# A hybrid attention layer on one core: another order of Strassen products, a last gate with priority, a plain last down-projection, and operands at equal addresses modulo 256

## The chip, the cores and the metric

The kernel runs on one core of a Trainium2 chip. A core has five engines with a queue of instructions each: TensorE (matmuls; the profile shows them as PE, and the loads of their stationary operands as PEld), VectorE (DVE), ScalarE (ACT), GpSimd (POOL, not used here) and SyncE (SP), whose queue issues the DMAs. They run side by side and wait for each other by semaphores. TensorE reads its two operands from SBUF, 128 partitions wide, and writes sums to PSUM, which has eight banks of 2 KB a partition.

The metric is the time of one execution on the device in microseconds; lower is better. One further execution was recorded by the hardware profiler, and every trace row is from that one.

## What is computed

One layer on 256 tokens of width 2048, in float32: RMS norm, an input projection, two kinds of attention with eight heads of 128 each, an output projection with a residual, then a gated feed-forward network (FFN) with a causal convolution of width 3 over the tokens. The change concerns the FFN, and the addresses in all of it:

```python
def conv_ffn(h, w_up_l, conv_w_l, conv_b_l, w_down_l):
    u = h @ w_up_l                        # 2048 -> 2 x 5632
    ...                                   # causal depthwise convolution, width 3, plus bias
    gate, val = jnp.split(u, 2, axis=-1)
    return (jax.nn.silu(gate) * val) @ w_down_l      # 5632 -> 2048

x = x + hybrid_mixer(h, ...)
x = x + conv_ffn(rms_norm(x, ffn_norm), ...)
```

## The kernel before

**Precision.** A float32 operand `a` is split into a high part `hi`, rounded to the matmul type `float32r`, and `lo = a - hi`. A product takes three matmuls: hi by hi, hi by lo, lo by hi. For weights, `split` (lines 204 to 213) makes `w_hi` with an ACT cast (line 208) and `w_lo` with a DVE subtraction (line 209). Every weight byte goes through both engines.

**The matmuls.** `token_major` (line 222) takes activations as the stationary operand, 128 tokens at a time, and 512 columns of weights as the moving one (lines 237 to 239). `feature_major` (line 244) takes the weights as stationary and `hT`, the normalized input transposed and split, as moving: for each of 16 slices of the input and two blocks of features one matmul of 512 columns (line 252, `hi` against both parts of `hT`) and one of 256 (line 257). It comes in two halves of eight slices, each with one load of 1 MB and one split. After each half it calls `step()`.

**The FFN.** 44 tiles of 128 features are worked on in six parts (line 40): four tiles in the first, eight in each of the others. A part goes through its tiles two at a time (lines 783 to 795): `up_pair` for the gate and for the value, each a `feature_major` and a `convolved` (line 596). `convolved` sums the PSUM parts (`t2`, lines 268 and 269), multiplies by the token factors into `up` (line 602), and forms the three taps: an ACT instruction (line 606) and two DVE ones (line 611) for each of the two tiles. Then silu (line 787), the product with the value (line 788), and the split of the result into `g2` (lines 790 and 791). One `g2` holds two tiles; a part of eight tiles has four pairs. From the third pair on, `combinations` (line 642) makes sums `s` of two pairs' gates on DVE and ACT.

**The down-projection of a part** is done while the next part's up-projections run. `down_in_seven` (line 664) is one step of Strassen's method in Winograd's form on blocks of four tiles by 512 columns and 128 tokens: seven products of 12 matmuls each (line 681) instead of eight, at the price of sums of weights on DVE (lines 719, 726, 732 and 743), of the activations (`s`), and of more additions to the residual (line 692). It is a generator; each `yield` ends a product. Its first product, `bank_c`, takes pairs 2 and 3 (the second half of the part's tiles), its second, `bank_a`, pairs 0 and 1, the others `s` of all pairs, the last pairs 2 and 3. Two such blocks cover 2048 columns. `step()` (line 621) hands them out: with a pace of 14 a half of an up-projection is followed by 14/16 of a product on average, the first product of a part coming after the second half. The first part has two pairs and goes through `down_plain` (line 749), the usual product of 24 matmuls for four tiles by 512 columns and both token blocks (lines 764 to 766, added at line 770).

**The last part** has no up-projection to run beside. Lines 803 to 806 deal out its down-projection by hand: `heavy`, seven products for columns 0 to 1023, and `light`, plain products for columns 1024 to 2047.

**Order.** TensorE's instructions run in the order in which they are written (`manual_schedule`, line 776). For the other engines a list scheduler fixes the order when the program is built; an instruction's place in the text is its priority, and `tc.high_priority(offset=n)` moves it ahead by `n` places. Weight loads and splits are moved ahead by `AHEAD` = 200, `t2`, the gate's product, `g2`, `combinations` and the residual's additions by 400. The instructions of `convolved` from line 602 on are not moved.

**Addresses.** Tiles lie in pools, one pool behind another, each tile rounded up to 32 bytes a partition. In the attention stage the pools behind `at` are `tmp`, `wraw`, `whi`, `wlo`, `late`; in the FFN the order is `wlo2`, `whi2`, `wraw2`, `wsum`, `ff`. Pools `at` and `wlo2` start at the same byte. The byte addresses of operands in a partition, before:

| tile | pool | address | modulo 256 | modulo 512 |
|---|---|---|---|---|
| `hT` (both stages; also holds `oT12` to `oT15`) | `big` | 37984 | 96 | 96 |
| `w_hi`, attention (first buffer; others 8192 on) | `whi` | 155424 | 32 | 288 |
| `w_lo`, attention | `wlo` | 171808 | 32 | 288 |
| `oT0` to `oT11` (attention outputs; steps of 2048) | `late` | 188192 | 32 | 288 |
| `w_lo`, FFN | `wlo2` | 73312 | 96 | 96 |
| `w_hi`, FFN | `whi2` | 97888 | 96 | 96 |
| `g2` (eight, steps of 4096) | `ff` | 179872 | 160 | 160 |
| `s` (two) | `ff` | 212640 | 160 | 160 |

Two things put them there: `lf`, 64 bytes in `at`, ahead of the pools behind it, with 128 bytes for `la` in `tmp`; and the two tiles `up`, 2080 bytes each, that lie in `ff` ahead of `t2`, the gates, `g2` and `s`. Slices of these operands are taken at multiples of 512 bytes, except in the three value projections of 344 columns, whose rows are 1376 bytes.

Of the kernel before, what the change touches and what calls it, by code (L numbers as in the profile page):

```python
# [2 lines left out]

# [40 lines left out]
def hybrid_layer(  # L44
# [227 lines left out]
    with ExitStack() as actx:  # L272
# [101 lines left out]
        step()  # L374

        vA = at.tile([P, NT, WF], F32, name="vA")
        lf = at.tile([P, NT, NH], F32, name="lf")
        for j in range(3):
            acc = project(2 * WF + 344 * j, 344)
            n = 344 if j < 2 else 336  # L380
# [197 lines left out]
    wraw = ctx.enter_context(tc.tile_pool(name="wraw2", bufs=4))  # L578
    wsum = ctx.enter_context(tc.tile_pool(name="wsum", bufs=1))
    ff = ctx.enter_context(tc.tile_pool(name="ff", bufs=2))  # L580
    psf = ctx.enter_context(tc.tile_pool(name="psf", bufs=2, space=bass.MemoryType.PSUM))
    crow = ff.tile([NC2, 4, P], F32, name="crow", tag="val", bufs=1)
    nc.sync.dma_start(crow[:, :3, :], conv_w[0].rearrange("w (n p) -> n w p", p=P))
    nc.sync.dma_start(crow[:, 3, :], conv_b[0].rearrange("(n p) -> n p", p=P))
    up = [ff.tile([P, 2, 2 + S], F32, name=f"up{i}", bufs=1) for i in range(2)]
    for u in up:
        dve.memset(u[:, :, 0:2], 0.0)
    n_up = 0
# [7 lines left out]
    def convolved(ps, f0, tag, bufs):  # L596

        nonlocal n_up
        u = up[n_up % 2]
        n_up += 1  # L600
        t2 = summed(ff, ps, "t2")
        dve.tensor_tensor(u[:, :, 2:], t2, R.unsqueeze(1).to_broadcast([P, 2, S]), op=ALU.mult)
        a = ff.tile([P, 2, S], F32, name=tag, tag=tag, bufs=bufs)
        for j in range(2):
            f = f0 + j
            act.activation(  # L606
                a[:, j, :], u[:, j, 2:], AF.Identity,
                scale=ccol[:, 2, f : f + 1], bias=ccol[:, 3, f : f + 1],
            )
            for w in range(2):  # L610
                dve.scalar_tensor_tensor(  # L611
                    a[:, j, :], u[:, j, w : w + S], ccol[:, w, f : f + 1], a[:, j, :],
                    op0=ALU.mult, op1=ALU.add,
                )
        return a
# [14 lines left out]
            else:  # L630
                n_behind -= 16

    def up_pair(f0, tag, bufs):

        nonlocal R
        acc = feature_major(wu, f0 * P, psa, "acc")
        if R is None:
            R = in_every_partition(dg2, 2, const)
            convolution_parameters()
        return convolved(acc, f0, tag, bufs)  # L640

    def combinations(g1, g2):

# [17 lines left out]
    def store(t, c0):  # L661
        nc.sync.dma_start(of[t * P : (t + 1) * P, c0 : c0 + 512], xt[t][:, c0 : c0 + 512])

    def down_in_seven(f0, pairs, sums, c0, final=False):


        w11, w12 = (rows_of(wd, f0, 4, c0 + i * 512, 512) for i in range(2))
# [15 lines left out]
                        stop=i == 3 and n == 2, skip_group_check=not first,  # L683
                    )

        adds = {}

        def add(t, half, bank, op=ALU.add):
            c = c0 + 512 * half
            to = xt[t][:, c : c + 512]  # L690
            with tc.high_priority(offset=2 * AHEAD):
                dve.tensor_tensor(to, to, bank, op=op)  # L692

            adds[t, half] = adds.get((t, half), 0) + 1
            if final and adds[t, half] == (1 if (t, half) == (1, 0) else 2):
                store(t, c)

        def ahead():
            return tc.high_priority(offset=AHEAD)

        bank_c = psb.tile([P, 512], F32, name="bank_c", tag="t")
        with ahead():
            parts = split(load(w21), 4, 512)
        product(bank_c, True, of_pairs(1, 0), parts)
        add(0, 0, bank_c)
        yield
        bank_a = psf.tile([P, 512], F32, name="bank_a", tag="a")
        with ahead():
            b11 = load(w11)
            parts = split(b11, 4, 512)  # L710
        product(bank_a, True, of_pairs(0, 0), parts)
        add(0, 0, bank_a)
        yield

        bank_b = psb.tile([P, 512], F32, name="bank_b", tag="t")
# [61 lines left out]
    for n_part, (f_lo, f_hi) in enumerate(FFN_PARTS):  # L777
        last_part = n_part == len(FFN_PARTS) - 1
        pairs, gates, sums = [], [], []
        n_behind = 0  # L780

        pace = 4 if n_part == 1 else 14
        for f in range(f_lo, f_hi, 2):
            gate = up_pair(f, "gate", 3)
            val = up_pair(NFT + f, "val", 1)
            with tc.high_priority(offset=2 * AHEAD):
                act.activation(gate, gate, AF.Silu)
                dve.tensor_tensor(gate, gate, val, op=ALU.mult)
                g2 = ff.tile([P, 2, 2, S], F32R, name="g2", tag="g2", bufs=8)
                act.copy(g2[:, 0], gate)  # L790
# [12 lines left out]
    heavy = down_in_seven(f_lo, pairs, sums, 0, final=True)  # L803
    light = down_plain(f_lo, pairs, 1024, 1024, final=True)
    for g in (light, heavy, light, heavy, heavy, light, heavy, heavy, heavy, light, heavy):
        next(g)


def _constants():
# [54 lines left out]
```

## Time and profile before

| | |
|---|---|
| time before, median of 3 runs | 1177.89 us (1177.38 to 1179.56) |
| the profiled execution | 1177.3 us, of which 1175.5 us from its first to its last instruction (the span) |
| granted TensorE clock over the span | 0.985 |
| busy: TensorE, VectorE, ScalarE | 1134.4, 906.3, 614.6 us |
| read from HBM, written | 217.80 MB, 2.10 MB (187 GB/s) |

A row of instructions in a list by time has its start and duration in us, the engine, the line, the operation, `out<-in` by the program's names, shapes, and how many follow each other; in brackets the idle time before it and what ended it. Times are from the span's start. Matmuls overlap, and a matmul's duration is a model's; the spacing of their starts tells the rate. A row of waits has the engine and line that waited, `<-` what it waited for, the total in us, how often, and the longest. In rows of groups the last columns are busy time, mean ns of one, and idle time before. "PEclk" is the granted share of TensorE's clock.

### The profile page before, as it was taken

What the parts mean: (1) busy time and instruction counts of PE and PEld (TensorE: products, weight loads), DVE (VectorE), ACT (ScalarE), POOL (GpSimd) and SP (SyncE); (2) the same over time, 40 slices, a digit from 0 to 9 for tenths busy, and PEclk for the clock granted to TensorE, in tenths of its full rate; (3) what the DMA queues carried; (4) which work ended last, traced back from release to release, by engine and by line L of the source; (5) the groups of instructions that cost most, each with busy time, mean ns of one, the idle gap of its engine ahead of it and who ended that gap; (6) DMA issues with size and microseconds to landing.
All of it is one profiled execution on the core that took longest, in us unless ns stands there. A gap on an engine that the chain in (4) does not pass through costs nothing.

```text
span 1175.5 us, 14481 instructions
## 1 busy us (share of the span) xinstructions
PE 1134.4 (97%) x5894; PEld 963.9 (82%) x5894; DVE 906.3 (77%) x982; ACT 614.6 (52%) x667; POOL 0.2 (0%) x4
## 2 busy tenths in 40 slices
PE   7999999999999989999999998999989998999967
PEld 5998888888888878888888887888878887888846
DVE  4646656455465676767899999989998999889985
ACT  5644445445563564554555565555545565555542
POOL 0000000000000000000000000000000000000000
PEclk9999999999999999999999999999989998999979
DMA  7665545554445395555557565575737566474732
GB/s 231 212 219 180 179 146 177 179 156 166 144 144 179 109 292 179 186 198 190 181 174 253 181 220 199 189 222 197 239 131 236 193 223 206 144 251 158 260 104 86
DMA packets 167292, 220.83 MB, mean 188 GB/s; under 512 B 3880, under 2 KB 117690, under 8 KB 167226
## 3 DMA queue, kind: packets, MB, share of 16 engines
q1 hardware_dynamic: 167226, 219.91, 57.6%
q8 instruction: 46, 0.75, 0.3%
q14 instruction: 20, 0.16, 0.0%
HBM read 217.80 MB, written 2.10 MB: 187 GB/s over the span
## 4 chain that ended last, share of the span: by engine, by line
PE 90%; DVE 4%; issue 2%; ACT 2%; DMA 1%; SPq 0%; ACTq 0%
PE pu L252 31%; PE pu L257 15%; PE bank_a L681 8%; PE acc L238 7%; PE acc L237 7%; PE acc L239 7%; PE bank_b L681 4%; PE bank_c L681 2%; DVE w_lo L209 2%; ACT w_hi L208 2%; PE bank_a L765 1%; PE bank_a L766 1%; PE bank_a L764 1%; DVE val L611 1%; PE acc L764 1%
## 5 line engine op out<-in xcount | busy, mean ns | idle before, releaser
L209 DVE TENSOR_TENSOR w_lo<-w_raw,w_hi 128x2048 fp32r<-128x2048 f32 (+2 forms) x204 | 449.3, 2206 | 193.2 <-ACT w_hi L208 192.7
L208 ACT CAST w_hi<-w_raw 128x2048 fp32r<-128x2048 f32 (+2 forms) x204 | 375.6, 1841 | 335.2 <-issue 137.4
L252 PE MATMUL pu<-hT,w_hi 128*128 128x512 f32 x1664 | 525.6, 397 | 1.0 <-DVE hT L154 0.9
L257 PEld LDWEIGHTS pu<-hT,w_lo 128*128 128x128 f32 x1664 | 313.9, 189 | 75.3 <-DVE w_lo L209 1.8
L257 PE MATMUL pu<-hT,w_lo 128*128 128x256 f32 x1664 | 328.9, 279 | 1.3 <-DVE w_lo L209 1.3
L252 PEld LDWEIGHTS pu<-hT,w_hi 128*128 128x128 f32 x1664 | 259.6, 190 | 7.3 <-DVE hT L154 1.4
L237 PE MATMUL acc<-w_hi,hT 128*128 128x512 f32 (+1 forms) x320 | 121.0, 378 | 0.0
L238 PE MATMUL acc<-w_lo,hT 128*128 128x512 f32 (+1 forms) x320 | 120.2, 376 | 0.3 <-DVE w_lo L209 0.3
L239 PE MATMUL acc<-w_hi,hT 128*128 128x512 f32 (+1 forms) x320 | 119.8, 374 | 0.0
L208 ACT CAST w_hi<-w_sum 128x2048 fp32r<-128x2048 f32 x27 | 51.6, 1912 | 86.7 <-PE pu L252 71.7
L209 DVE TENSOR_TENSOR w_lo<-w_sum,w_hi 128x2048 fp32r<-128x2048 f32 x27 | 61.8, 2290 | 10.0 <-ACT w_hi L208 9.7
L238 PEld LDWEIGHTS acc<-w_lo,hT 128*128 128x128 f32 x320 | 60.5, 189 | 10.5 <-DVE w_lo L209 1.1
L239 PEld LDWEIGHTS acc<-w_hi,hT 128*128 128x128 f32 x320 | 60.4, 189 | 10.0
L237 PEld LDWEIGHTS acc<-w_hi,hT 128*128 128x128 f32 x320 | 60.5, 189 | 9.3
L681 PE MATMUL bank_c<-w_hi,g 128*128 128x512 f32 x72 | 28.9, 455 | 24.1 <-ACT g L790 24.1
L681 PE MATMUL bank_a<-w_hi,s 128*128 128x512 f32 x144 | 49.3, 404 | 2.2 <-DVE x L692 2.2
L681 PE MATMUL bank_b<-w_hi,s 128*128 128x512 f32 x144 | 48.2, 395 | 0.0
L681 PE MATMUL bank_a<-w_hi,g 128*128 128x512 f32 x144 | 48.1, 395 | 0.0
L611 DVE SCALAR_TENSOR_TENSOR val<-up,ccol,val 128x256 f32<-128x256 f32 x88 | 39.6, 480 | 1.7 <-ACT val L606 1.3
L681 PEld LDWEIGHTS bank_c<-w_hi,g 128*128 128x128 f32 x72 | 15.2, 213 | 29.6 <-ACT g L790 25.9
L611 DVE SCALAR_TENSOR_TENSOR gate<-up,ccol,gate 128x256 f32<-128x256 f32 x88 | 38.0, 479 | 0.8 <-ACT gate L606 0.7
L237 PE MATMUL acc<-w_hi,oT 128*128 128x512 f32 x96 | 38.0, 396 | 0.0
(186 smaller groups left out, 1195.4 us busy)
## 6 DMA issues: line engine op xcount, KB each, us to landing
w_raw<-in_w_up_dram SPq DMA_DIRECT2D x88, 1024.0 KB, 5.2
w_raw<-in_w_down_dram SPq DMA_DIRECT2D x53, 1024.0 KB, 5.0
w_raw<-in_w_in_dram SPq DMA_DIRECT2D x36, 1024.0 KB, 5.2
w_raw<-in_w_out_dram SPq DMA_DIRECT2D x16, 1024.0 KB, 5.0
w_raw<-in_w_in_dram SPq DMA_DIRECT2D x12, 688.0 KB, 4.0
w_raw<-in_w_in_dram SPq DMA_DIRECT2D x8, 512.0 KB, 3.9
out_dram<-x SPq DMA_DIRECT2D x8, 256.0 KB, 2.4
x<-in_x_dram SPq DMA_DIRECT2D x3, 512.0 KB, 6.3
```

The lines of the kernel that those rows point to most:

```text
L208: act.copy(hi[:, :n], raw[:, :n])
L209: dve.tensor_tensor(lo[:, :n], raw[:, :n], f32(hi[:, :n]), op=ALU.subtract)
L237: nc.tensor.matmul(o, lhi, hi[:, i, :], start=first, stop=False)
L238: nc.tensor.matmul(o, lhi, lo[:, i, :], start=False, stop=False)
L239: nc.tensor.matmul(o, llo, hi[:, i, :], start=False, stop=last)
L252: nc.tensor.matmul(acc[:, j, :], hi[:, i, j * P : (j + 1) * P], hT[:, k].rearrange("p a b -> p (a b)"), start=k == 0, stop=False,)
L257: nc.tensor.matmul(acc[:, j, S:], lo[:, i, j * P : (j + 1) * P], hT[:, k, 0, :], start=False, stop=k == KT - 1,)
L611: dve.scalar_tensor_tensor(a[:, j, :], u[:, j, w : w + S], ccol[:, w, f : f + 1], a[:, j, :], op0=ALU.mult, op1=ALU.add,)
L681: nc.tensor.matmul(bank, lhs(a, l, j), r[:, i, :], start=first and i + n == 0, stop=i == 3 and n == 2, skip_group_check=not first,)
L764: nc.tensor.matmul(acc[t], g[:, 0, ts], hi[:, i, :], start=first, stop=False)
L765: nc.tensor.matmul(acc[t], g[:, 0, ts], lo[:, i, :], start=False, stop=False)
L766: nc.tensor.matmul(acc[t], g[:, 1, ts], hi[:, i, :], start=False, stop=last)
```

## The change

Four things. In `down_in_seven` the second product (`bank_a`, pairs 0 and 1) and the first (`bank_c`, pairs 2 and 3) change places. `convolved` of the last pair of each part, for the gate and the value, is put at a priority 400 places ahead. The last part's down-projection is plain for all 2048 columns, in two blocks of 1024; of each block's two halves the first four tiles come first. And two tiles change place: `lf` is given twice the space, of which half is used, and the `up` tiles move to a pool of their own behind `ff`.

```diff
-        lf = at.tile([P, NT, NH], F32, name="lf")
+        lf = at.tile([P, 2, NT, NH], F32, name="lf")[:, 0]
...
     ff = ctx.enter_context(tc.tile_pool(name="ff", bufs=2))
+    fu = ctx.enter_context(tc.tile_pool(name="fu", bufs=1))
...
-    up = [ff.tile([P, 2, 2 + S], F32, name=f"up{i}", bufs=1) for i in range(2)]
+    up = [fu.tile([P, 2, 2 + S], F32, name=f"up{i}") for i in range(2)]
...
-    def up_pair(f0, tag, bufs):
+    def up_pair(f0, tag, bufs, soon):
...
-        return convolved(acc, f0, tag, bufs)
+        with tc.high_priority(offset=2 * AHEAD) if soon else nullcontext():
+            return convolved(acc, f0, tag, bufs)
...
-        bank_c = psb.tile([P, 512], F32, name="bank_c", tag="t")
-        with ahead():
-            parts = split(load(w21), 4, 512)
-        product(bank_c, True, of_pairs(1, 0), parts)
-        add(0, 0, bank_c)
-        yield
         bank_a = psf.tile([P, 512], F32, name="bank_a", tag="a")
         with ahead():
             b11 = load(w11)
             parts = split(b11, 4, 512)
         product(bank_a, True, of_pairs(0, 0), parts)
         add(0, 0, bank_a)
+        yield
+        bank_c = psb.tile([P, 512], F32, name="bank_c", tag="t")
+        with ahead():
+            parts = split(load(w21), 4, 512)
+        product(bank_c, True, of_pairs(1, 0), parts)
+        add(0, 0, bank_c)
         yield
...
-            gate = up_pair(f, "gate", 3)
-            val = up_pair(NFT + f, "val", 1)
+            gate = up_pair(f, "gate", 3, f == f_hi - 2)
+            val = up_pair(NFT + f, "val", 1, f == f_hi - 2)
...
-    heavy = down_in_seven(f_lo, pairs, sums, 0, final=True)
-    light = down_plain(f_lo, pairs, 1024, 1024, final=True)
-    for g in (light, heavy, light, heavy, heavy, light, heavy, heavy, heavy, light, heavy):
-        next(g)
+
+    for c in (0, 1024):
+        halves = [down_plain(f_lo, pairs, c + i * 512, 512, final=True) for i in range(2)]
+        for g in halves + halves:
+            next(g)
```

By the sizes of the tiles, `w_hi`, `w_lo` and `oT0` to `oT11` of the attention stage move up by 64 bytes (96 modulo 256, 352 modulo 512) and `g2` and `s` of the FFN move down by 4160 (96 modulo 256 and modulo 512); `hT` and the FFN's weights stay at 96. The stores and the count of additions that `down_in_seven` kept for its last use (`final`, `adds`) go with it; `down_plain` stores its columns itself (line 772).

More of the change, by code (lines that the diff above doesn't have):

```diff
@@ L1 @@
 from collections import deque
-from contextlib import ExitStack
+from contextlib import ExitStack, nullcontext
 import concourse.bass as bass
@@ L662, in store, with down_in_seven @@
         nc.sync.dma_start(of[t * P : (t + 1) * P, c0 : c0 + 512], xt[t][:, c0 : c0 + 512])
-    def down_in_seven(f0, pairs, sums, c0, final=False):
+    def down_in_seven(f0, pairs, sums, c0):
         w11, w12 = (rows_of(wd, f0, 4, c0 + i * 512, 512) for i in range(2))
@@ L684, in product @@
                     )
-        adds = {}
         def add(t, half, bank, op=ALU.add):
@@ L692, in add @@
                 dve.tensor_tensor(to, to, bank, op=op)
-            adds[t, half] = adds.get((t, half), 0) + 1
-            if final and adds[t, half] == (1 if (t, half) == (1, 0) else 2):
-                store(t, c)
         def ahead():
             return tc.high_priority(offset=AHEAD)
-        bank_c = psb.tile([P, 512], F32, name="bank_c", tag="t")
-        with ahead():
-            parts = split(load(w21), 4, 512)
-        product(bank_c, True, of_pairs(1, 0), parts)
-        add(0, 0, bank_c)
-        yield
         bank_a = psf.tile([P, 512], F32, name="bank_a", tag="a")
```

## The prediction

> **What bounds the kernel now.** I read the page first, then the waits of TensorE, then the busy time by stretches.
>
> ```profile
> span 1175.5 us, 14481 instructions
> PE 1134.4 (97%) x5894; PEld 963.9 (82%) x5894; DVE 906.3 (77%) x982; ACT 614.6 (52%) x667; POOL 0.2 (0%) x4
> PEclk9999999999999999999999999999989998999979
> ...
> PE bank_c L681 <- ACT g L790: 24.1, 4, 10.5
> ```
>
> TensorE is busy for 97% of the span, so what counts is where it stops and how fast it streams. It stops in one place: four times `bank_c`, the first product of a Strassen block, waits for the last pair's `g2` (cast at line 790), 24.1 us in all, 10.5 of them once; the other three make 24.1 - 10.5 = 13.6, or 4.5 each. The clock row falls to 8 in the slices of these waits. What one looks like, in order of time on TensorE:
>
> ```profile
> 987.01 0.40 PE L681 MATMUL bank_c<-w_hi,g 128*128 128x512 f32 x1
> ...
> 988.17 0.40 PE L681 MATMUL bank_c<-w_hi,g 128*128 128x512 f32 x1
> 993.10 0.80 PE L681 MATMUL bank_c<-w_hi,g 128*128 128x512 f32 x1 [4.53 <-ACT g L790]
> ```
>
> The product runs six matmuls on the third pair, then stands 4.53 us for the fourth, and its next matmul takes 0.80 us, twice the usual 0.40: the clock is at half. VectorE shows why `g2` is late:
>
> ```profile
> 977.77 0.68 DVE L269 TENSOR_TENSOR t<-pu,t 128x512 f32<-128x512 f32 x1
> 978.37 2.28 DVE L209 TENSOR_TENSOR w_lo<-w_raw,w_hi 128x2048 fp32r<-128x2048 f32 x1
> 980.57 1.66 DVE L611 SCALAR_TENSOR_TENSOR gate<-up,ccol,gate 128x256 f32<-128x256 f32 x4
> ...
> 985.99 2.28 DVE L719 TENSOR_TENSOR w_sum<-w_raw 128x2048 f32<-128x2048 f32 x1
> 988.20 0.87 DVE L611 SCALAR_TENSOR_TENSOR val<-up,ccol,val 128x256 f32<-128x256 f32 x2
> ...
> 992.42 0.62 ACT L790 CAST g<-gate 128x512 fp32r<-128x512 f32 x1 [3.50 <-DVE gate L788]
> ```
>
> The last convolution starts at 977.77 and its result is cast at 992.42. In between, 2.28 us weight splits and a weight sum go first. Last, the load by stretches (columns: length, then busy time of PE, PEld, DVE, ACT, POOL with counts, granted clock):
>
> ```profile
> 722.40:857.30 134.90, 130.31 (x681) 110.33 (x681) 126.19 (x122) 75.26 (x66) 0.00 (x0) 0.98 0.62 204
> 857.30:993.10 135.80, 131.28 (x681) 111.14 (x681) 126.10 (x121) 75.39 (x66) 0.00 (x0) 0.98 0.61 201
> ...
> 864.00:988.00 124.00, 124.00 (x659) 105.47 (x658) 114.73 (x105) 70.32 (x61) 0.00 (x0) 1.00 0.63 206
> 920.00:988.00 68.00, 68.00 (x361) 57.76 (x361) 66.40 (x63) 38.59 (x34) 0.00 (x0) 1.00 0.64 210
> ```
>
> The first two rows are the parts between stalls. VectorE is busy 126 of 135 us in each, 66.40 of 68.00 in the second half of a part. It is the next bound, and close.
>
> **The part boundaries.** The waits are 13.6 us. Around them the clock costs more: a part's matmuls are 16 half up-projections and 14 products of 12 matmuls.
>
> ```profile
> 550.10 0.63 PE L252 MATMUL pu<-hT,w_hi 128*128 128x512 f32 x2
> ...
> 555.68 0.62 PE L252 MATMUL pu<-hT,w_hi 128*128 128x512 f32 x2
> ...
> 731.24 2.79 PE bank_a L681 x12
> ```
>
> Eight groups of four matmuls take 5.58 us (0.6975 each), which is one half; a product takes 2.80. So a part's own work is 16 x 5.58 + 14 x 2.80 = 128.5 us. The first part row has 134.9 - 128.5 - 4.5 = 1.9 us beyond work and wait, the second 2.8; giving the third boundary 2.8 too, the clock costs 7.5 us and the three boundaries 21.1.
>
> With `bank_a` first, `bank_c`'s matmuls on the fourth pair come one product and one half later, 2.80 + 5.58 = 8.4 us, against a wait of 4.53: the order alone covers it, and the priority, which puts the multiply at line 602 and the taps at 606 and 611 of the last gate and value ahead of the splits, adds cover. No instruction is added. What is moved is about 2 x (0.60 + 4 x 0.40) = 4.4 us of VectorE's work and four activations, past splits on both engines; behind them wait TensorE's next halves. `b11` now keeps its load buffer through one more product; four such buffers are there, so SP's queue runs less far ahead:
>
> ```profile
> w_raw<-in_w_down_dram SPq DMA_DIRECT2D x53, 1024.0 KB, 5.0
> ```
>
> A load lands in 5.0 us. I cost the longer hold at nothing, covered by the 8.4 us in which TensorE uses two loads; without that cover the next half is late by at most 5.0.
>
> What is late next is VectorE. Each boundary, 21.1 / 3 = 7.0 us, was time in which it went on working. From 864 to 988 it stands 124.00 - 114.73 = 9.3 us, of which only 1.6 after 920: 7.7 us early in the part, when its buffers are full. So a lag of 7 can be made up by 920, but before that it meets the first thin reserves:
>
> ```profile
> 983.00:1003.00 20.00, 15.47 (x69) 12.72 (x69) 18.68 (x20) 8.05 (x11) 0.00 (x0) 0.83 0.43 145
> ...
> 863.79 2.29 DVE L209 TENSOR_TENSOR w_lo<-w_raw,w_hi 128x2048 fp32r<-128x2048 f32 x1
> ...
> 868.66 2.29 DVE L209 TENSOR_TENSOR w_lo<-w_sum,w_hi 128x2048 fp32r<-128x2048 f32 x1 [1.99 <-ACT w_hi L208]
> ...
> 870.01 0.40 PE L257 MATMUL pu<-hT,w_lo 128*128 128x256 f32 x2
> ```
>
> The split that ends at 863.79 + 2.29 = 866.1 is first read at 870.0: 3.9 us in reserve. A lag of 7.0 overdraws this by 3.1, or by 1.8 if the 20.00 - 18.68 = 1.3 us that VectorE idled around the stall (first row) are saved; afterwards idle times like the 1.99 at 868.66 pay it back. So each boundary gives back between 0 (the new order wastes less) and 4.7 (3.1, and 1.6 of slow clock as below). I take the middle, 2.5, at each and the clock once: 21.1 - 7.5 - 1.6 = 12.0 us gained.
>
> **The last down-projection.** From its first matmul to its last:
>
> ```profile
> 1111.83 0.39 PE L764 MATMUL acc<-w_hi,g 128*128 128x512 f32 x1
> ...
> 1155.76 0.48 PE L681 MATMUL bank_a<-w_hi,s 128*128 128x512 f32 x1 [2.21 <-DVE x L692]
> ...
> 1159.72 0.40 PE L681 MATMUL bank_a<-w_lo,s 128*128 128x512 f32 x1
> ...
> 1171.15 0.39 PE L681 MATMUL bank_a<-w_hi,g 128*128 128x512 f32 x1
> 1171.58 0.69 DVE L692 TENSOR_TENSOR x<-x,bank_a 128x512 f32<-128x512 f32 x1 [1.51 <-PE bank_a L681]
> ```
>
> The last row is the final add; the store after it ends the span. The stage lasts 1171.38 - 1111.83 = 59.55 us for 84 + 96 = 180 matmuls, 42.0 us of work at 2.80 for 12. It holds the 10.5 us wait, the 2.21 us wait of a product for a bank that VectorE was still adding, and slow clock after both. Plain products need 4 x 48 = 192 matmuls, 2.8 us more, and no bank is used twice. The last pair is needed 60 matmuls in, after 14.0 us; before, it came 5.6 + 1.4 + 10.5 = 17.5 us in. The 3.5 us are found: four weight sums of 2.28 go from VectorE, two of them in the chain of waits ahead of the last taps, and the taps have priority:
>
> ```profile
> 1116.55 2.29 DVE w_sum L719
> ...
> 1122.70 2.20 DVE w_raw L732
> ...
> L656 DVE TENSOR_TENSOR s<-t,s 128x512 fp32r<-128x512 f32 x20 | 13.1, 688 | 1.8 <-ACT s L655 1.6
> L650 DVE TENSOR_TENSOR t<-gate 128x256 f32<-128x256 f32 x10 | 4.2, 422 | 0.2
> ```
>
> The combinations of the last part stay, unused: four of 0.42 and two of 0.69 us, 3.1 on VectorE, for the last pair, hidden under those 14 us. Loads fall from nine to eight, stores stay eight; the tail is the same add and store. So 192 x 0.2333 = 44.8 us, or 43.5 at the faster spacing below: a gain of 14.75 to 16.0; I take 16.0.
>
> After a wait as short as 2.21 us the ten matmuls from 1155.76 to 1159.72 took 3.96 us instead of 2.33, so 1.6 were lost to the clock. The Trainium skill, "TensorE: Matmul & The Clock Gate", section "What's actually happening", lets the clock fall after an idle window of about 3.4 us; by that the 2.5 us waits at the boundaries would cost no clock and the gain there would be 21.1 - 7.5 = 13.6, while by the row it would be 13.6 - 3 x 1.6 = 8.8. The forecast's one slow stretch lies between.
>
> **The addresses.** Before, the attention stage's `w_hi` and `w_lo` lie 64 bytes below `hT` modulo 256, and equal to `oT`; FFN products read `g2` and `s` 64 above `w_hi`. The same lines run on both kinds:
>
> ```profile
> 367.82 0.39 PE L237 MATMUL acc<-w_hi,oT 128*128 128x512 f32 x1
> ...
> 372.58 0.40 PE L237 MATMUL acc<-w_hi,hT 128*128 128x512 f32 x1
> ...
> 377.95 0.39 PE L239 MATMUL acc<-w_hi,hT 128*128 128x512 f32 x1
> ...
> L239 PE MATMUL acc<-w_hi,hT 128*128 128x512 f32 x224 | 89.1, 398 | 0.0
> ```
>
> Equal: 21 matmuls from 367.82 to 372.58, 0.2267 us each. Unequal: 23 from 372.58 to 377.95, 0.2335. Same shape, same line, neighbours in time: 6.8 ns. All row-wise 512-column matmuls become equal. In attention that is 3 x 224 = 672 (lines 237 to 239 in like number), 4.6 us. But there `w_hi` and `hT` will differ by 256 modulo 512, which no row shows, while `g2`, `s` and `w_hi` become equal modulo 512, like `oT`. Against it: the column-wise projections. In the FFN they have equal addresses already and take 0.6975 a group; in attention, unequal:
>
> ```profile
> 178.09 0.62 PE L252 MATMUL pu<-hT,w_hi 128*128 128x512 f32 x2
> ...
> 181.54 0.62 PE L252 MATMUL pu<-hT,w_hi 128*128 128x512 f32 x2
> ```
>
> Five groups in 3.45 us, 0.690. Their 128 groups may lose 1.0 us. Attention: 3.6 gained, bounds -1.0 and 4.6. FFN products outside the last stage: 96 + 4 x 168 = 768, 5.2 us; the 96 in part 1 (0.65) count in full, the rest, 4.6, half, 2.3, since there VectorE sets the pace in turns.
>
> The Trainium skill, the same page, section "Step-by-step: what each phase is for", says: "Loading the next tile's weights doesn't steal SBUF read bandwidth from the running matmul." By that no address could matter and the terms of this part would be nothing; the two spacings above speak against it. It is the second rival.
>
> **The sum.** 12.0 + 16.0 + 3.6 + 0.65 + 2.3 = 34.55 us. The profiled execution took 1177.3 us, 1.8 outside its span, 0.6 under the median of 1177.89. On the median's scale: 1177.9 - 34.55 = 1143.35; I say 1143.5.
>
> **The rivals.** (1) Everything comes back: no lag, all spacings: 21.1 + 16.0 + 4.6 + 5.2 = 46.9 us, 1131. For it: 7.7 us of VectorE's idle per part; against: the reserves of 3.9. (2) Addresses do nothing, `oT` being quick by its place or size alone: 12.0 + 14.75 = 26.75, 1151. For it: equal addresses show no gain in the column-wise groups. (3) VectorE takes the place of the wait: its idle 7.7 us a part stays, so a part can't be under 126.1 + 7.7 = 133.8, 1.6 less than the 135.4 mean; 3 x 1.6 + 16.0 + 3.6 + 0.65 = 25.1, 1152.8. For it: 66.40 of 68.00; against: that idle is waiting for buffers that TensorE frees, which it then frees sooner. (4) Slower: the prioritized taps stand at the head of VectorE's and ScalarE's queues before their `pu` is done, the splits behind them come late, and TensorE stops at the ends of five parts, clock at half. A stop must eat 34.55 / 5 = 6.9 us each to decide; at 9 (a wait of 6 and 3 of clock) it is 1143.4 + 45 = 1188. Against: `t` at line 269 has that priority already and caused no wait. (5) The priority changes no order and the chain stays late: the order and the last stage still gain, little behind the forecast: if each boundary keeps 1 us more, 1146.5.
>
> **Chances.** Forecast 0.45; (1) 0.15; (2) 0.14; (3) 0.17; (4) 0.04; (5) 0.05. The bounds reach from 1131 (all gains) to 1157.1: boundaries at 21.1 - 14.1 = 7.0, last stage at 14.75, attention -1.0, sum 20.75. Range 1130.5 to 1156. About 0.2% is what a measurement here can tell from no change: faster 0.95, same 0.01, slower 0.04.
>
> **What would show it.** TensorE's waits list no `bank_c` on line 790; the clock row is 9 through the FFN; a part lasts 128 to 131 us; the last stage about 43.5 us from the first to the last matmul; 12 matmuls of a product 2.72 us instead of 2.80; line 237 on `hT` at 0.2267. New rows "PE ... <- DVE w_lo L209" early in a part would show the lag. Wrong would be a wait of several us on `w_lo` at every part's end, or spacings of 0.2335 throughout.

## The result, and the profile after

The change takes the median from 1178.09 to 1159.93 us (1159.1 to 1162.79, four runs; the kernel before 1177.38 to 1179.56): a ratio of 0.9849, 95% interval 0.9829 to 0.9868. The forecast was 1143.5, its range 1130.5 to 1156. So 18.2 us came of some 34.5 that were forecast.

The page of the kernel after: span, busy time of the engines, granted clock in 40 slices.

```profile
span 1157.7 us, 14490 instructions
PE 1123.5 (97%) x5906; PEld 964.0 (83%) x5906; DVE 888.9 (77%) x972; ACT 608.2 (53%) x664; POOL 0.2 (0%) x4
PEclk9999999999999999999999998999999999999999
```

TensorE's waits in the kernel after (engine and line that waited, what for, total us, times, longest):

```profile
PE pu L252 <- DVE t L269: 13.4, 3, 4.5
PE acc L760 <- DVE t L269: 4.5, 1, 4.5
```

The wait of `bank_c` for `g2` is gone, as forecast. Two new rows stand in its place: four times 4.5 us for `t`, the sum of the two PSUM parts of an up-projection. Here are the four on TensorE's timeline (start, duration, and in brackets the idle time before):

```profile
705.27 1.19 PE L252 MATMUL pu<-hT,w_hi 128*128 128x512 f32 x2 [4.47 <-DVE t L269]
...
839.98 1.19 PE L252 MATMUL pu<-hT,w_hi 128*128 128x512 f32 x2 [4.47 <-DVE t L269]
...
969.10 0.39 PE L683 MATMUL bank_a<-w_hi,g 128*128 128x512 f32 x1
973.95 1.08 PE L252 MATMUL pu<-hT,w_hi 128*128 128x512 f32 x2 [4.47 <-DVE t L269]
...
1107.48 0.76 PE L760 MATMUL acc<-w_hi,g 128*128 128x512 f32 x1 [4.47 <-DVE t L269]
...
1152.34 0.39 PE L762 MATMUL acc<-w_hi,g 128*128 128x512 f32 x1
1152.76 1.29 DVE L766 TENSOR_TENSOR x<-acc,x 128x512 f32<-128x512 f32 x2 [4.15 <-PE acc L762]
```

They stand at the very start of a part (the first matmul of its first gate), and at the start of the last down-projection. From one to the next, 134.7, 134.0 and 133.5 us pass. A part's own work is now 16 halves of 5.58 and 14 products of 2.72 us, 127.4; with the wait of 4.47, 1.7 to 2.9 us are left for the slow clock after it and smaller losses. After the wait two matmuls take 1.08 or 1.19 us, where a pair at full clock takes 0.63.

Where the profiled execution's time went, by four points on TensorE's timeline:

| | before | after | gained | forecast |
|---|---|---|---|---|
| to the FFN's first matmul | 414.5 | 411.7 | 2.8 | 3.6 |
| from there to the last stage's first matmul | 697.3 | 695.8 | 1.5 | 14.95 (12.0 + 0.65 + 2.3) |
| from there to the last matmul | 59.32 | 44.86 | 14.5 | 16.0 |
| from there to the end of the span | 4.35 | 5.4 | -1.0 | 0 |

The first point varies by some 2 us: in the ten traces of this case with the new addresses it lies between 411.5 and 413.2 (mean 412.4), in the four with the old ones between 414.1 and 414.9 (mean 414.4), so 2.1 us are gained there on average. Most of the miss lies in the second row, the parts: 13.5 us of 16.7. Why TensorE waits for `t` is seen ahead of the third of these waits, on TensorE (first line), VectorE and ScalarE:

```profile
949.78 0.39 PE L257 MATMUL pu<-hT,w_lo 128*128 128x256 f32 x2
...
959.14 1.27 DVE L612 SCALAR_TENSOR_TENSOR val<-up,ccol,val 128x256 f32<-128x256 f32 x3
960.33 2.29 DVE L209 TENSOR_TENSOR w_lo<-w_sum,w_hi 128x2048 fp32r<-128x2048 f32 x1
...
965.43 0.48 DVE L612 SCALAR_TENSOR_TENSOR val<-up,ccol,val 128x256 f32<-128x256 f32 x1
965.94 0.69 DVE L784 TENSOR_TENSOR gate<-gate,val 128x512 f32<-128x512 f32 x1
966.67 0.42 DVE L652 TENSOR_TENSOR t<-gate 128x256 f32<-128x256 f32 x1
...
971.32 1.29 DVE L658 TENSOR_TENSOR s<-t,s 128x512 fp32r<-128x512 f32 x2
972.04 1.19 ACT L268 COPY t<-pu 128x512 f32<-128x512 f32 x2 [0.21 <-DVE s L658]
...
973.12 1.28 DVE L269 TENSOR_TENSOR t<-pu,t 128x512 f32<-128x512 f32 x2
```

Read it from below. The two sums at 973.12 are those of the last pair's gate and value, which empty the two PSUM buffers of the up-projections; TensorE can't begin a new part until the first of them, the gate's, is done. The gate's product had been ready since its last matmuls at 949.78, 22 us before it is copied: the copy waits not for TensorE but for `s` at line 658 (bracket at 972.04). `summed` and `combinations` take their tiles from one tag, `t2`, with two buffers. The third pair's `combinations` fill both at 966.67 and free them only when `s` is formed at 971.32 and later. And they are late since the third pair's taps (959.14 and 965.43) have no priority and stand among the weight splits.

In the kernel before, the same order held and cost nothing:

```profile
960.52 0.42 DVE L650 TENSOR_TENSOR t<-gate 128x256 f32<-128x256 f32 x1
...
966.98 1.29 DVE L656 TENSOR_TENSOR s<-t,s 128x512 fp32r<-128x512 f32 x2
...
970.99 0.68 DVE L269 TENSOR_TENSOR t<-pu,t 128x512 f32<-128x512 f32 x1
...
975.85 0.62 PE L252 MATMUL pu<-hT,w_hi 128*128 128x512 f32 x2
```

There `s` is done at 968.3, the gate's sum at 971.7, and TensorE comes to the new part only at 975.85, four us later. The stall for `g2` kept TensorE behind and gave VectorE the time. Without it TensorE is at this place at 969.5, 6.4 us sooner, while `s` is done at 972.6, 4.3 us later than before.

### The profile page after: what moved, and what is told of

Same layout as the page of the kernel before. It is cut to its first block, busy times and chain, and to the rows that moved or that the text cites. A ratio compares the mean times of both kernels' runs of the same rounds, so it can differ in the third digit from the quotient of the medians.

```text
span 1157.7 us, 14490 instructions
## 1 busy us (share of the span) xinstructions
PE 1123.5 (97%) x5906; PEld 964.0 (83%) x5906; DVE 888.9 (77%) x972; ACT 608.2 (53%) x664; POOL 0.2 (0%) x4
## 4 chain that ended last, share of the span: by engine, by line
PE 92%; DVE 3%; ACT 2%; DMA 1%; issue 1%; SPq 0%; DVEq 0%; ACTq 0%
PE pu L252 33%; PE pu L257 16%; PE acc L238 7%; PE acc L237 7%; PE acc L239 7%; PE bank_a L683 7%; PE bank_b L683 4%; PE bank_c L683 2%; ACT w_hi L208 2%; DVE w_lo L209 2%; PE acc L760 1%; PE acc L761 1%; PE acc L762 1%; PE bank_a L760 1%; PE bank_a L761 1%
## 5 line engine op out<-in xcount | busy, mean ns | idle before, releaser
L252 PE MATMUL pu<-hT,w_hi 128*128 128x512 f32 x1664 | 528.5, 399 | 14.4 <-DVE t L269 13.4
L208 ACT CAST w_hi<-w_sum 128x2048 fp32r<-128x2048 f32 x24 | 45.9, 1914 | 79.9 <-DVE w_sum L715 43.4
L209 DVE TENSOR_TENSOR w_lo<-w_sum,w_hi 128x2048 fp32r<-128x2048 f32 x24 | 54.9, 2290 | 3.2 <-ACT w_hi L208 2.8
L683 PE MATMUL bank_a<-w_hi,g 128*128 128x512 f32 x128 | 42.1, 390 | 0.0
L683 PE MATMUL bank_b<-w_hi,s 128*128 128x512 f32 x128 | 42.1, 390 | 0.0
L683 PE MATMUL bank_a<-w_hi,s 128*128 128x512 f32 x128 | 42.1, 390 | 0.0
L268 ACT COPY t<-pu 128x512 f32<-128x512 f32 x52 | 30.2, 580 | 15.1 <-PE pu L257 14.2
L237 PE MATMUL acc<-w_hi,oT 128*128 128x512 f32 x96 | 38.0, 396 | 0.0
L239 PE MATMUL acc<-w_hi,oT 128*128 128x512 f32 x96 | 37.5, 390 | 0.0
```

Of the source, the lines that this page charges most:

```text
L208: act.copy(hi[:, :n], raw[:, :n])
L209: dve.tensor_tensor(lo[:, :n], raw[:, :n], f32(hi[:, :n]), op=ALU.subtract)
L237: nc.tensor.matmul(o, lhi, hi[:, i, :], start=first, stop=False)
L239: nc.tensor.matmul(o, llo, hi[:, i, :], start=False, stop=last)
L252: nc.tensor.matmul(acc[:, j, :], hi[:, i, j * P : (j + 1) * P], hT[:, k].rearrange("p a b -> p (a b)"), start=k == 0, stop=False,)
L268: act.copy(t2, acc[:, :, S:])
```

## The experiments

Two theories stood against each other. Theory S, the shared buffer: the wait for `t` is there because `combinations` holds the buffer that the last gate's sum needs, and it goes when the sum has a place of its own. Theory V, rival 3 of the prediction: VectorE sets the length of a part (133.8 us at least), and whatever wait is taken away, another comes for the same time. V's number fits the parts of the kernel after: 134.0 and 133.5. Each kernel below was timed beside the kernel before (medians 1176.9 to 1179.55), and ratios are to that.

**A place of its own for the sum.** In `convolved` the sum goes straight into the buffer `up`, which the next instruction fills in any case. VectorE and ScalarE execute as many instructions as before, 972 and 664.

```diff
-        t2 = summed(ff, ps, "t2")
-        dve.tensor_tensor(u[:, :, 2:], t2, R..., op=ALU.mult)
+        with tc.high_priority(offset=2 * AHEAD):
+            act.copy(u[:, :, 2:], ps[:, :, S:])
+            dve.tensor_tensor(u[:, :, 2:], ps[:, :, :S], u[:, :, 2:], op=ALU.add)
+        dve.tensor_tensor(u[:, :, 2:], u[:, :, 2:], R..., op=ALU.mult)
```

> The changed kernel, with the sum of the PSUM parts written straight into `up`, so that `convolved` takes no buffer of the tag that `combinations` uses. Theory S (shared buffer): TensorE's 4.5 us waits at the four part ends come from the last gate's sum waiting for the third pair's combinations; they go, with their slow clock, 6.1 to 7.4 us each, 26 in all: 1134, a part's period falls from 134 to 128. Theory V (VectorE's load): a part can't be under its 126.3 us of busy time and 7 of idle; the wait moves to another row and the time stays within 4 us of 1160.

Measured: 1146.38 us (1144.49 to 1147.21), ratio 0.9724, interval 0.9707 to 0.974; 13.5 us less than after. Its waits:

```profile
PE bank_a L685 <- DVE w_lo L209: 4.8, 3, 1.6
...
PE bank_c L685 <- DVE w_lo L209: 2.0, 3, 0.8
```

No row for `t` is left. On VectorE the last gate's sum now stands here, and the next part begins 14.5 us after its end, at 965.3:

```profile
950.13 0.68 DVE L604 TENSOR_TENSOR up<-pu,up 128x512 f32<-128x512 f32 x1
```

The stretch of one part (columns as in the prediction: length, busy time of PE, PEld, DVE, ACT, POOL, clock):

```profile
854.00:984.70 130.70, 128.22 (x682) 109.36 (x682) 125.50 (x121) 74.61 (x66) 0.00 (x0) 1.00 0.63 209
```

A part takes 130.7 us at full clock with the same work on VectorE, 3 us under the floor of theory V. So the cause of the wait is the one that S names, and V's floor falls: VectorE was busy for 126 of 134 us in the kernel after, and in part of the other 8 us it could have worked. But S forecast 1134 and a part of 128, a gain of 26 us where 13.5 came. V's forecast, within 4 us of 1160, is missed as well. S had nothing come in the wait's place, and here V is right by half: a part lost 6.7 us beyond its own 127.4 in the kernel after and still loses 3.3, with waits for `w_lo` that were not there.

**The same edit in the kernel before.**

> The kernel before, and in it only the rows' sum written into the buffer of the up-projection instead of a buffer t. Theory S (the buffer t shared with the weight-side sums takes the wait's place once the wait for the gate is gone, and costs nothing as long as that wait stands): TensorE still waits 4.9 to 10.7 us for g2 at the first product of each part, so the time stays within 0.4% of before, 1173 to 1180, and what own_t2 gained over after (13.5 us) is not found here. Rival: the shared buffer costs the same 4.5 us and its clock wherever it stands, then some 6 us at each of the part ends are gained here too, 1155 to 1165.

Measured: 1182.38 us, ratio 1.0033, interval 1.0019 to 1.0048: within the 0.4% given, on the slow side, though over the 1180 given, as the kernel before took 1179.55 beside it.

```profile
PE bank_c L683 <- ACT g L792: 28.6, 4, 10.5
```

So the shared buffer cost nothing while the wait for `g2` stood; freeing it made that wait 4.5 us longer in sum (24.1 before). The expectation of no change was low by some 3 us: the sums that now come earlier go ahead of the chain to `g2`, an explanation that is argued, not tried. The rival, 1155 to 1165, falls.

**The priority.** First the kernel after without it, then the kernel after with it for every pair, then the kernel with the sum's own place and no priority.

```diff
-        with tc.high_priority(offset=2 * AHEAD) if soon else nullcontext():
+        with tc.high_priority(offset=2 * AHEAD) if False else nullcontext():
```

> The changed kernel without the priority of the last pair's convolutions. Theory S: the late step is the third pair, which never had the priority, so nothing of the wait goes: 1160, same rows of waits. Theory V: the same time too, the wait perhaps on another row. A third view, that the priority itself made the new wait by pushing other work back, gives 4 x 6 us less: 1136.

Measured: 1159.39 us, ratio 0.9843, interval 0.9828 to 0.9858, as the kernel after, with the same rows of waits for `t`, 13.4 us in three and 4.5 in one. Both theories said so, and the third view, 1136, falls. While the gate's sum waits for its buffer, putting what follows it first does nothing.

```diff
-        with tc.high_priority(offset=2 * AHEAD) if soon else nullcontext():
+        with tc.high_priority(offset=2 * AHEAD) if True else nullcontext():
```

> The changed kernel with the priority for the convolutions of every pair. Theory S: the third pair's taps no longer lag, its combinations come some 6 us earlier (its last taps stood at 959 to 966, up to 15 us behind their matmuls), and the 4.5 us waits go: 1134 to 1140. Theory V: the same load, so the wait moves to the weight splits and the time stays at 1155 to 1162.

Measured: 1183.43 us, ratio 1.0045, interval 1.003 to 1.006. It missed both ranges, and by far.

```profile
PE bank_a L683 <- DVE w_lo L209: 22.0, 8, 4.1
PE bank_b L683 <- DVE w_lo L209: 6.9, 5, 2.4
```

The wait for `t` is gone here too, but TensorE waits 28.9 us for weight splits. One of them on VectorE, and then TensorE:

```profile
882.91 2.28 DVE L722 TENSOR_TENSOR w_sum<-w_sum,w_raw 128x2048 f32<-128x2048 f32 x1
885.12 1.66 DVE L612 SCALAR_TENSOR_TENSOR val<-up,ccol,val 128x256 f32<-128x256 f32 x4
886.70 2.28 DVE L728 TENSOR_TENSOR w_raw<-w_raw 128x2048 f32<-128x2048 f32 x1
888.90 0.68 DVE L784 TENSOR_TENSOR gate<-gate,val 128x512 f32<-128x512 f32 x1
889.50 2.28 DVE L209 TENSOR_TENSOR w_lo<-w_sum,w_hi 128x2048 fp32r<-128x2048 f32 x1
...
891.84 0.80 PE L683 MATMUL bank_a<-w_lo,s 128*128 128x512 f32 x1 [4.09 <-DVE w_lo L209]
```

All four taps, 1.66 us, go ahead of a split that TensorE needs at 887.75 (the matmul starts 4.09 us late); but so do the next weight sum, 2.28 us, and the gate's product, 0.68, and VectorE does not stand still. So the taps alone are not the 4.09 us: the whole order has moved against the splits. That is near rival 4, which was given a chance of 0.04 at 1188 for the change itself: splits behind prioritized work come late. Its prioritized taps that hold a queue while they wait for their `pu` do not show here. That the change escapes this because only one pair in four is moved is argued, not tried with two or three.

> The run own_t2 without the priority of the last pair's convolutions. If the priority brings `g2` in time once the buffer is free, its lack puts a wait for `g2` back, 2 to 6 us a part: 1154 to 1170. If the order alone covers it, as the forecast said, the same as own_t2 within 3 us: 1143 to 1149, perhaps less, with less pushed back.

Measured: 1149.46 us (1149.03 to 1153.97), ratio 0.9777, interval 0.9753 to 0.98.

```profile
PE acc L762 <- ACT g L788: 3.0, 1, 3.0
```

It is just over the range for the order alone, and far under that for a wait for `g2` in every part. With the buffer free the priority is worth 3 us by the medians and 6 by the ratios, whose intervals don't overlap, and the largest single piece stands in this row: without it the last stage waits 3.0 us for the last pair, and takes 48.3 us instead of 44.3. The prediction had counted on priority and fewer weight sums there. No `bank_c` waits for `g2`: in the parts the order alone is enough.

**The order.** The first edit is the kernel before with the change's order of the products alone (the two paragraphs of `bank_a` and `bank_c` change places); the second is the kernel with the sum's own place, with `bank_c` first again.

> The kernel before with `bank_a` first and nothing else. Theory S: the wait for `g2` turns into the 4.5 us wait for `acc` at the part ends, 6.5 us each with the clock, so the three boundaries gain 0 to 1.5 us; in the last stage the first wait shrinks only if the product of pairs 0 and 1 covers it. 1173 to 1178. If the new order alone recovered its waits (the forecast's step), 1157 or less.

Measured: 1171.74 us, ratio 0.9955, interval 0.9939 to 0.9971.

```profile
PE pu L252 <- DVE t L269: 13.2, 3, 4.4
PE acc L764 <- DVE t L269: 4.4, 1, 4.4
```

The exchange of one wait for the other is made by the order alone. It takes 1.3 us less than the range given: the stretch from the FFN's first matmul to the last stage grows, from 697.3 to 700.9 us, but the last stage falls from 59.3 to 49.1, as its 10.5 us wait gives way to one of 4.4 ahead of it.

> own_t2 with the product of the second block first again, priority and all else kept. If the priority alone brings the last pair's combinations in time for it, the time stays that of own_t2, 1144 to 1149, and no wait for g2 is at bank_c. If the order carries the gain, as the prediction has it, TensorE waits for g2 at the first product of three parts, some 4 to 7 us each with its clock: 1156 to 1168.

Measured: 1143.8 us (1142.3 to 1145.01), ratio 0.9699, interval 0.9685 to 0.9714. Its largest wait in the FFN:

```profile
PE bank_b L685 <- DVE w_lo L209: 3.6, 2, 1.9
```

No wait for `g2`: with a buffer of its own, the priority brings the last pair in time even for the old order. That the order carries the gain was wrong for this kernel: against the wait for `g2` in the parts either the order or the priority is enough, and having both isn't told apart from the priority alone (the two intervals overlap). Two of its parts take 127.3 us: with no wait a part is as short as its own work.

**The other parts of the change alone**, each in the kernel before: the two moved tiles; and the plain last down-projection.

```diff
+        lf = at.tile([P, 2, NT, NH], F32, name="lf")[:, 0]
...
+    up = [fu.tile([P, 2, 2 + S], F32, name=f"up{i}") for i in range(2)]
```

> The kernel before with the addresses alone changed (`lf` widened, `up` in its own pool). Both theories: attention 2.7 us and the first parts 0.7 to 1.8 less, as the changed kernel shows, 1.2 in the last stage. Theory V: within the parts that end in a stall nothing, 1173.5. Theory S: there the products' 1.1 us a part count too: 1170.

Measured: 1171.87 us, ratio 0.9954, interval 0.9938 to 0.997: 6.0 us less. The two forecasts, 1173.5 and 1170, lie on either side, so this run does not tell the theories apart. The `bank_c` waits stay (26.2 us in four, 2.1 more than before). The line that showed the two spacings before, on `hT`:

```profile
371.81 0.39 PE L237 MATMUL acc<-w_hi,hT 128*128 128x512 f32 x1
...
376.57 0.39 PE L237 MATMUL acc<-w_hi,hT 128*128 128x512 f32 x1
```

That is 21 matmuls in 4.76 us, 0.2267 each, where they took 0.2335 before, with nothing changed but the addresses.

> The kernel before with the plain last stage and nothing else. The three boundary waits stay, since the blocks before keep their order; the last stage falls from 59.6 us to 192 x 0.2335 = 44.8 if it waits for nothing: 1163. If it begins with the wait for `acc` as in the changed kernel, 6 us more: 1169.

Measured: 1167.42 us, ratio 0.9924, interval 0.9903 to 0.9945: 9.5 us less.

```profile
PE bank_c L681 <- ACT g L790: 13.9, 3, 4.9
...
PE acc L766 <- DVE g L791: 1.7, 1, 1.7
```

The 10.5 us wait is gone and the last stage waits 1.7 us for the last pair, without the priority. There is no wait for `t` in front of it here: it comes with the new order only. The time lies between the two that were forecast. The last stage takes 48.1 us, not 44.8: the wait, and half clock for most of the 4.2 us after it (a granted clock of 0.59 there).

**What is left: VectorE's lag.** The kernel with the sum's own place still loses 3.3 us a part, most of it in waits for `w_lo` (1.6 and 0.8 us). One of the weight sums, `w` plus `b22`, is left out in the kernel below, so two of 2.28 us per part; its products are done as before.

```diff
-            dve.tensor_tensor(w, w, b22, op=ALU.add)
```

> The run own_t2 without the weight sum w + b22 of each Strassen block (line 726 of the kernel before; the output differs), 2 x 2.2 us of VectorE's work a part. If the waits left in own_t2, about 3.2 us a part on `w_lo` at bank_c and bank_a, are VectorE's lag, the 1.75 us ones go and the rest shrink: 2 to 3 us a part less, 1136 to 1140. If they come from ScalarE or the loads, 1146 again.

Measured: 1141.0 us (1139.93 to 1141.28), ratio 0.9694, interval 0.9679 to 0.971. The waits of 1.6 us at `bank_a` are gone, and a part, from the matmul behind one `bank_c` to the next, takes 129.3 us instead of 130.7:

```profile
PE pu L257 <- DVE w_lo L209: 3.6, 5, 1.4
PE bank_b L685 <- DVE w_lo L209: 3.4, 4, 0.9
```

So 4.6 us less work on VectorE give 1.4 us a part, less than the 2 to 3 expected, and the time is 1 us over the range given; the rest of the lag only moves to later places.

Two edits then tried to relieve VectorE with the full result: `best` is the kernel with the sum's own place and without the last part's unused `combinations`; `best_gp` also puts the four first sums of each set of `combinations` on GpSimd.

```diff
-                if len(pairs) > 2:
+                if len(pairs) > 2 and not last_part:
```

> own_t2 without the six combinations of activations that the last part makes and its plain down-projection does not read. The theory: VectorE is behind in the last part, so some 3.9 us of its work less there take away what is left of TensorE's waits at the end of that part, 1142 to 1146. Rival: TensorE waits for nothing there by now, then 1146, as own_t2.

Measured: 1143.17 us (1142.87 to 1145.47), ratio 0.9699, interval 0.9685 to 0.9713. It isn't told apart from the kernel it comes from (0.9724, 0.9707 to 0.974): the intervals overlap. In the traces the parts are alike and the last stage is 1.0 us shorter (43.3). With the run that has `bank_c` first again it is the fastest kernel here that computes everything, 3% under before and 1.5% under the change.

```diff
-        dve.tensor_tensor(t5, a21, a22, op=ALU.subtract)
+        nc.gpsimd.tensor_tensor(t5, a21, a22, op=ALU.subtract)
...
```

> best, with four of the subtractions on the weight or activation side of each set of sums on GpSimd instead of VectorE. Theory L (the 3 us that own_t2 still loses at the start of each part are VectorE's lag with the weight splits): VectorE has some 3 us less in each set, the waits of bank_a and bank_c for w_lo shrink, 1136 to 1143. Rival: GpSimd is several times slower on them than VectorE or holds up VectorE's reads, the combinations come later than before and bank_c waits for them: 1150 to 1175.

Measured: 1154.77 us, ratio 0.9795, interval 0.978 to 0.981: the rival's time, though no `bank_c` waits for the combinations. Four queues in order of time:

```profile
698.08 2.63 POOL L654 TENSOR_TENSOR t<-gate 128x256 f32<-128x256 f32 x1 [114.53 <-DVE gate L786]
...
702.13 0.62 ACT L659 CAST s<-t 128x512 fp32r<-128x512 f32 x1 [3.57 <-POOL t L655]
...
703.27 0.69 DVE L604 TENSOR_TENSOR up<-pu,up 128x512 f32<-128x512 f32 x1 [3.16 <-ACT up L603]
...
710.81 0.79 PE L257 MATMUL pu<-hT,w_lo 128*128 128x256 f32 x2 [2.90 <-DVE w_lo L209]
```

GpSimd takes 2.63 us for the first subtraction, which VectorE does in 0.42. It runs beside a weight split on VectorE, from 697.83 to 700.11, and ends 0.6 us after it; the next three, with VectorE idle, take 0.73 to 0.74 us each. So it is in the whole trace: of the 32 subtractions and additions on GpSimd the twelve that took over 1 us all ran beside an instruction of VectorE, and no one that ran alone took over 0.75. ScalarE's cast stands waiting for GpSimd, the copy of the next up-projection stands behind the cast, VectorE idles 3.16 us for the copy, and its next split comes 2.90 us late for TensorE. VectorE had less work (872.9 us busy, 880.3 in `best`) and was later.

## Why the prediction came out as it did

**What was wrong.** The step "What is late next is VectorE", with its reserve read from one `w_lo`, priced the boundaries at a lag of 2.5 us each and a gain of 12.0 us. It looked only at weight splits. The chain of the last gate, whose own sum at line 269 it had set down as "has that priority already and caused no wait", takes a buffer from the tag that `combinations` uses; the prediction never asked who else holds it. This put a wait of 4.47 us and its slow clock at each of three boundaries and ahead of the last stage, and of the 14.95 us forecast up to there 1.5 came. "The order alone covers it" was right of `g2` in the parts, and is what the kernel with the sum's own place and no priority shows; what it uncovered was one step upstream. The prediction's sign of being wrong, several us on `w_lo` at every part's end, had the place right and the tile wrong.

With that wait taken away, the prediction's own terms come out to about 1 us, but for attention. The same four points in the kernel with the sum's own place, from its timeline: first matmul of the FFN at 412.6, the rest from these rows:

```profile
1095.85 0.39 PE L762 MATMUL acc<-w_hi,g 128*128 128x512 f32 x1
...
1140.17 0.39 PE L764 MATMUL acc<-w_hi,g 128*128 128x512 f32 x1
```

The parts take 1095.85 - 412.6 = 683.3 us where before took 697.3: 14.0 gained, against a forecast of 14.95. That this is so near is in part luck: in the first part TensorE waits 1.95 us here for `hT` (0.95 in the kernel before) and runs slow after it, which takes 2.7 us, and the parts behind it gain 16.7. The last stage takes 44.3 instead of 59.3: 15.0 against 16.0. And 1146.38 stands 2.9 us from the 1143.5 forecast, within its range; 0.9 is lost at the tail, and attention gives some 1.5 us less than its 3.6.

**Point by point.** (a) `bank_c` waits for `g2` are gone: right. (b) Clock row at 9 through the FFN: one slice of 8 is left. (c) A part of 128 to 131 us: wrong (134.7, 134.0 and 133.5), right with the buffer free (130.7). (d) A last stage of 43.5 us: 45.1 (44.86, and 0.23 for the last matmul), after a wait of 4.47 that no term had; the excess of 1.6 is slow clock behind that wait: the seven matmuls from 1107.48 to 1110.61 take 3.13 us, 1.59 at full spacing. The last pair itself was in time, as forecast: no row waits for `g2` there. (e) Addresses: a product takes 2.72 us, as forecast; 6.0 us for the addresses alone, against 3.6 + 0.65 + 2.3 = 6.55. That the sums are so near is in part luck: in that run's trace attention gave 1.3 us (2.1 in the mean of all traces) of 3.6, the stretch to the last stage 3.6 where 2.95 were forecast, and 0.9 came in the last stage, which this sum leaves out. (f) The tail was called "the same add and store": it is 1.0 longer, 0.6 of it since two adds follow the last matmul (1.29 us at 1152.76, instead of 0.69). (g) The lag of VectorE at `bank_c` in the parts, 0.8 us, and at `bank_a`, 1.6, is there as forecast, 3.3 us a part where 2.5 and a slow stretch at one boundary were taken, but appears only once the wait for `t` is gone.

**The rivals.** Rival 1, everything comes back, falls: even with the buffer free a part loses 3.3 us. Rival 3 had the right size for a part and the wrong cause: 133.8 us as a floor of VectorE's work, where the kernel with the sum in a place of its own ran 130.7 with the same work. A length that fits is no cause. Rival 2 falls by the address run. Rival 5, the priority without effect, holds for the kernel as changed, but because of the buffer, and doesn't explain the time: the term it took away was 3 us. Something near rival 4 comes with the priority on every pair, and not in the kernel after. Forecast and rivals together had a chance of 1.00: nothing was left for a wait that none of them names, which is what came.

## What to carry to other kernels

Before you price a wait's removal, follow each instruction ahead of it back to the buffers it takes, and list everything else that draws from the same tag: a dependency that costs nothing today may have its cover in the very stall you remove. When a part then comes out at a length that fits a saturated engine, test that with the same work and one buffer more, and expect the engine's lag to take back a part of the gain. And a priority moves only what is ready, so free the buffer first and then see whether order or priority is still needed.

## What the runs showed of the hardware

**Spacing and addresses.** The 512-column matmuls with activations as the stationary operand start 0.2267 us apart when both operands lie at addresses equal modulo 256, and 0.2335 when they lie 64 bytes apart, on the same line and shape. In attention after the change `w_hi` and `hT` differ by 256 modulo 512 and the spacing is 0.2267 all the same, so the modulus that counts here is 256 or a divisor of it, and no divisor of 64. With the weights stationary and equal addresses the effect is the reverse. In attention, a group of four (two of 512 columns, two of 256) took 0.690 us before with unequal addresses and takes 0.698 now; from the kernel after:

```profile
176.42 0.64 PE L252 MATMUL pu<-hT,w_hi 128*128 128x512 f32 x2
...
180.61 0.63 PE L252 MATMUL pu<-hT,w_hi 128*128 128x512 f32 x2
```

That is six groups in 4.19 us, the loss that the prediction bounded at 1.0 us for 128 groups. Why a few bytes do this, no run shows. The Trainium skill, "TensorE: Matmul & The Clock Gate", section "Step-by-step: what each phase is for", holds that loading the next weights takes no read bandwidth from the running matmul. It says nothing there of addresses: that none could matter was the prediction's reading of it, and the 6.0 us speak against that reading. Whether the weight load's reads are what the addresses change, no run shows.

**Clock after a short wait.** The length of a wait does not decide alone whether the clock falls. Granted clock in stretches that begin with the end of a wait (columns as above, the clock being the third figure from the end); the first two are the kernel with GpSimd, then the plain last stage alone, then the sum's own place in the kernel before:

```profile
710.80:714.30 3.50, 3.49 (x11) 3.10 (x12) 3.50 (x5) 0.86 (x1) 0.00 (x0) 0.50 0.63 209
844.50:848.00 3.50, 3.48 (x20) 3.08 (x21) 3.50 (x5) 0.87 (x1) 0.00 (x0) 1.00 0.68 213
...
1129.00:1133.20 4.20, 4.19 (x11) 3.32 (x12) 1.59 (x4) 0.62 (x1) 0.00 (x0) 0.59 0.00 0
...
1159.90:1163.40 3.50, 3.47 (x15) 2.86 (x16) 2.48 (x2) 0.35 (x1) 0.00 (x0) 1.00 0.00 0
```

The first two follow waits of 2.90 and 2.89 us of the same matmul, on the same line and shape: half clock after one, full after the other. The third follows 1.73 us, the fourth 2.22, at the place where the prediction had read a loss of 1.6 us behind 2.21. Over the fourteen traces, of TensorE's waits over 1 us behind the first 30 us, none of the 35 up to 1.70 us was followed by less than full clock in the next 5 us; of the 17 from 1.73 to 2.89 us 12 were, with 0.66 to 0.70 on average, which makes 3.0 to 3.4 us at half clock; and all 32 from 2.90 us on were. So the prediction's 1.6 us behind one wait was a draw and not a rule. What decides between 1.73 and 2.89, no run shows. The Trainium skill, "TensorE: Matmul & The Clock Gate", section "What's actually happening", puts the idle window after which the clock falls at about 3.4 us; here waits from 1.73 us on were followed by half clock.
